# A hybrid decoder layer in float32: the second recurrence column's weights asked for one projection sooner, and two groups of ScalarE instructions bound behind that column's rounding

## The chip, the cores and the metric

The kernel runs on one core of a Trainium2 chip. The metric is the device time of one execution in microseconds; the median of three executions before the change is 1988.41 us (1987.54, 1988.41 and 1988.47).

The engines work side by side and synchronize by semaphores: PE multiplies matrices (and loads weights, PEld), DVE (VectorE), ACT (ScalarE) and POOL (GpSimd) work on elements, SP (SyncE) issues most of the transfers, POOL some. Each engine takes its instructions strictly in its own order: one that waits holds up all that stand behind it there.

## The reference

One layer of a decoder trunk over 1024 tokens and 16 meta tokens, width 1024, in float32:

```python
h = h + 0.5 * swiglu(rms_norm(h, ffn1_norm[l]), ffn1_w_in[l], ffn1_w_out[l])
u = rms_norm(h, mix_norm[l]) @ w_in[l]
hq, hf, hi, hg, sq, sk, sv = jnp.split(u, ...)
o_hg = hgrn2(hq, hf, hi, hg, lb_all[l], hgrn_out_norm[l], valid)
o_sb = stick_breaking(sq, sk, sv, sb_q_norm[l], sb_k_norm[l], valid)
h = h + jnp.concatenate([o_hg, o_sb], axis=-1) @ w_out[l]
h = h + 0.5 * swiglu(rms_norm(h, ffn2_norm[l]), ffn2_w_in[l], ffn2_w_out[l])
```

What matters here is the projection by `w_in`. Its columns feed a gated linear recurrence with four heads of 128 (query, forget gate, value and output gate) and a stick-breaking attention with eight heads of 64, whose queries and keys are normalized by head:

```python
q = rms_norm(split_heads(q_raw, SB_HEADS), q_gain)
k = rms_norm(split_heads(k_raw, SB_HEADS), k_gain)
z = jnp.einsum('bhqd,bhkd->bhqk', qblk, k) * scale
log_beta = jnp.where(allowed, jax.nn.log_sigmoid(z), -jnp.inf)
log_keep = jnp.where(allowed, jax.nn.log_sigmoid(-z), 0.0)
suffix = lax.cumsum(log_keep, axis=3, reverse=True) - log_keep
w = jnp.exp(log_beta + suffix)
```

## The kernel before

**Products.** A float32 operand is held as two: an upper part, rounded by a cast, and a lower part, the rest. A product is three matmuls (upper by upper, lower weights by upper, upper weights by lower; lines 248 to 250). For a block of 128 columns of `w_in`, `col_tile` and `split_w` issue one transfer on SP (line 226, tile `raw`, two buffers), round it on ScalarE (line 231, `wh`, three buffers) and form the lower part on VectorE (line 233, `wl`, three buffers). The rounding is the `wh` cast; this text calls it the column's rounding.

**The stage.** The attention heads are projected in four pairs, `sb_project` with p from 0 to 3: keys, values and queries of a pair, each in chunks of up to 512 tokens. `sb_qk` then normalizes the pair's queries and keys: squares on ScalarE and sums on VectorE (lines 1424 to 1427), the roots, the products on GpSimd (line 1438), transposes back on VectorE (line 1444), and for each of four pieces `put_split`: the upper part `ohi` on ScalarE (line 1375), the lower part `olo` on VectorE (line 1376), and two writes to DRAM issued by GpSimd (lines 1379 and 1380). `ohi` and `olo` have three buffers each, so the fourth piece waits for the write of the first.

**The recurrence's columns.** `hgrn_fill` projects sixteen columns, for each of four heads in the order v, f, q, g. The first two (v and f of head 0) are computed right behind the fourth pair, in four pieces of 264, 264, 256 and 256 tokens; the others are woven into the attention. A piece of v is copied out by ScalarE (line 1108), a piece of f goes through two sigmoids (lines 1114 and 1115) and two scalings on VectorE (lines 1116 and 1119), a half of q or g through one sigmoid and a product (lines 1122 and 1123). All are staged in the tile `st`, four buffers, and stored by SP (lines 1110, 1120 and 1124). Two PSUM banks take turns for the projections up to f, and one serves from q on.

**The scores.** `sb_jobs` and `sb_scores` work on one head after the other. For a piece of the scores, PE forms `z` (lines 1599 to 1602; two banks), ScalarE takes two sigmoids, `keep` and `sig` (lines 1605 and 1606), VectorE scans `keep` (line 1609) and GpSimd multiplies (line 1615). The tiles of the scores lie in memory that the fourth pair's tiles leave; a first write to such a tile waits for the last reader of what lay there.

**What sets the order.** PE's order is written out by hand (the weaving of `weave` and `braid`). The other engines' instructions are placed by a scheduler from when it expects them to be ready; `issue_after(ins)` binds the instructions of its block that run on the engine of `ins` behind `ins` in that engine's order, without a wait for its end. `project` asks for weights up to two columns ahead (`self.columns`, lines 1069 to 1075) and keeps each rounding in `self.rounds`. The list ends with the first column of the recurrence, so that one's weights are asked for during the fourth pair's value projection. From there `hgrn_fill` asks for one column ahead, when a column begins (line 1134): the second column at the start of the first, the third at the start of the second, and so on. `kept["round"]` (line 1135) is the rounding traced last, and the first column's copies stand behind it (line 1142). The fourth pair's upper parts stand behind `self.rounded`, the rounding traced last when their piece is traced (line 1447).

Of the kernel before, what the change touches and what calls it, by code (L numbers as in the profile page):

```python
# [40 lines left out]
class Block:  # L41
# [1050 lines left out]
    def hgrn_fill(self, xh, xl, pool, dst):  # L1092

        nc = self.nc
        plan, cols = self.heads_plan, self.columns_of_heads()

        def staged(n):
            return pool.tile([P, 512], F32, tag="st", name="st", bufs=4)[:, :n]

        def use(kind, h, ps, c0, n):  # L1100
            s = slice(c0, c0 + n) if kind in "vf" else slice(c0 - META, c0 - META + n)
            t = staged(n)
            if c0 >= HALVES[1][0] and kind != "g":
                ps = ps[:, ::-1]
                at = s.start + HALVES[1][0] + T - 2 * c0 - n
                s = slice(at, at + n)
            if kind == "v":
                nc.scalar.copy(t, ps)  # L1108
                with self.tc.issue_after(self.last_load.ins):
                    nc.sync.dma_start(dst[kind][h, :, s], t)  # L1110
                return
            elif kind == "f":
                k = staged(n)
                nc.scalar.activation(t, ps, AF.Sigmoid)
                nc.scalar.activation(k, ps, AF.Sigmoid, scale=-1.0)
                nc.vector.tensor_scalar(
                    t, t, self.lbc[:, h : h + 1], self.lb[:, h : h + 1], ALU.mult, ALU.add
                )
                nc.vector.tensor_scalar_mul(k, k, self.lbc[:, h : h + 1])
                nc.sync.dma_start(dst["k"][h, :, s], k)  # L1120
            else:
                nc.scalar.activation(t, ps, AF.Sigmoid)
                nc.vector.tensor_mul(t, t, ps)
            nc.sync.dma_start(dst[kind][h, :, s], t)

        def weights(i):
            return self.col_tile(self.a["w_in"][0], cols[i])

        kept = {"next": None}

        def part(i, ci, c0, n, half):
            if ci == 0 and half == 0:
                kept["w"] = kept["next"] or self.ahead_w.pop(cols[0])
                kept["next"] = weights(i + 1) if i + 1 < len(plan) else None
                kept["round"] = self.rounded.ins
            if half == 0:
                kept["ps"] = self.proj_bank(n)
            self.product(
                kept["ps"], kept["w"], xh, xl, c0, n, range(4 * half, 4 * half + 4)
            )  # L1140
            if half == 1:
                with self.tc.issue_after(kept["round"]) if i == 0 else ExitStack():
                    use(*plan[i], kept["ps"], c0, n)

        for i, (kind, _) in enumerate(plan):
            for ci, (c0, n) in enumerate(PIECES if kind in "vf" else HALVES):
                for half in range(2):
                    yield 12 * (n * 0.42 + 13), lambda a=(i, ci, c0, n, half): part(*a)
# [177 lines left out]
    def sb_project(self, p, xh, xl, pool, mix, dst):  # L1326
        nc = self.nc
        vT = pool.tile([P, T], F32, tag="vTs", name="vTs", bufs=2)
        kT = pool.tile([P, T + META], F32, tag="kT", name="kT", bufs=2)
        nc.gpsimd.memset(kT[:, T:], 1.0)  # L1330
        qT = pool.tile([P, SEQ], F32, tag="qT", name="qT", bufs=2)
        def use_q(ps, ci, c0, n):
            s = slice(c0 - META, c0 - META + n)
            nc.scalar.copy(qT[:, s], ps)

        def use_k(ps, ci, c0, n):
            nc.scalar.copy(kT[:, c0 : c0 + n], ps)

        def use_v(ps, ci, c0, n):
            nc.scalar.copy(vT[:, c0 : c0 + n], ps)  # L1340

        w = None
        if p == 0:
            w, self.ahead_w, self.rounds = self.early_w, {}, {}
            self.columns = [c + P * i for i in range(1, 4) for c in (2560, 3072, 2048)]
            self.columns.append(self.columns_of_heads()[0])
            for use, x, ci in ((use_k, "k", 0), (use_v, "v", 1), (use_v, "v", 2), (use_v, "v", 0),
                               (use_k, "k", 1), (use_k, "k", 2)):
                use(self.early[x][ci], ci, *CHUNKS[ci])
            use_q(self.early["q"][0], 0, *CHUNKS[0])  # L1350
            self.after_early()
        else:
            yield from self.project(xh, xl, 2560 + P * p, CHUNKS, use_k)
            yield from self.project(xh, xl, 3072 + P * p, CHUNKS, use_v)
        done = [self.sb_v(p, vT, mix, dst[2]), self.sb_qk(p, qT, kT, pool, mix, dst)]
        rest = self.project(xh, xl, 2048 + P * p, HALVES[: 1 if p == 0 else 2], use_q, w)
        if p == 0:
            yield next(rest)
        yield "start", done[0]
        yield from rest  # L1360
        yield "start", done[1]
        return done
# [47 lines left out]
    def sb_qk(self, p, qT, kT, pool, mix, dst):  # L1410
# [31 lines left out]
        for src, c0, b0, nb in rows:  # L1442
            t = src[:, c0 : c0 + 32 * nb]
            nc.vector.transpose(t, nat[:, b0 : b0 + nb].rearrange("p b d -> p (b d)"))
            n = min(32 * nb, (SEQ if src is qT else T) - c0)
            gain, to = (self.qg8, dst[0]) if src is qT else (self.kg, dst[1])
            with self.tc.issue_after(self.rounded.ins) if p == 3 else ExitStack():
                self.put_split(to, p, slice(c0, c0 + n), t[:, :n], mix, gain)
            yield 0, 1500

# [888 lines left out]
```

## Time and profile before

| | |
|---|---|
| median of three executions | 1988.41 us (1987.54 to 1988.47) |
| the profiled execution, device time | 1989.4 us |
| its span, from the first instruction to the last | 1987.7 us |
| granted TensorE clock, mean over the span | 0.998 |
| HBM read and written | 233.75 MB and 111.38 MB |
| 835 to 865 us: busy PE, DVE, ACT, POOL of 30 us | 28.52, 14.42, 13.49, 7.08 |
| 860 to 895 us: busy PE, DVE, ACT, POOL of 35 us | 27.25, 24.14, 21.76, 12.91 |
| 895 to 1180 us: busy PE, DVE, ACT, POOL of 285 us | 276.68, 200.22, 171.65, 106.34 |

Times within the span count from its first instruction. A row of the timeline has start, duration, engine, line, operation, the tile written and the tile read, and in brackets how long the engine was idle before it and what ended that. A wait is put down to the one that came last. The span and the device time differ by 1.7 us in the profiled execution; differences of the span can be carried over to the device time.

The stage of the change lies between 800 and 905 us. The fourth pair's values are projected up to 826 us, its queries up to 837.5, the v column from there on, the f column up to 862.3, and the first scores follow.

### The profile page before, as it was taken

The numbers are of one execution on the slowest core, as the hardware profiler recorded it, in microseconds if no ns is written. First come the engines' busy times: TensorE is split into PE (matmuls) and PEld (weight loads), VectorE is DVE, ScalarE is ACT, GpSimd is POOL, SyncE is SP. The second block draws the span as 40 slices with busy tenths as digits, with TensorE's granted clock in tenths as the row PEclk, the third lists the DMA queues.
The fourth block names the chain that finished last, engine by engine and source line by source line (L and its number), as shares of the span: only waits on it lengthen the run. The fifth ranks groups of instructions, "written<-read, shape, count | busy, mean of one in ns | idle before, by whom it ended". The sixth has DMA issues, their size and how long they took to land.

```text
span 1987.7 us, 30439 instructions
## 1 busy us (share of the span) xinstructions
PE 1938.9 (98%) x10768; PEld 1631.7 (82%) x10768; DVE 1390.3 (70%) x2176; ACT 854.7 (43%) x1719; POOL 449.4 (23%) x616
## 2 busy tenths in 40 slices
PE   7999999999999999989999999899999999999998
PEld 6888888888888888878898978787888888888887
DVE  7977777877677765567777676567566766767774
ACT  6523443334444444456666635433233332344443
POOL 3010100010000003133333332220544544520000
PEclk9999999999999999999999999999999999999999
DMA  7366887758966225664454176665523323278463
GB/s 209 92 169 166 254 272 242 238 183 317 374 207 185 93 73 150 154 191 135 127 152 117 58 264 184 149 228 181 185 96 106 107 96 111 102 266 301 122 197 138
DMA packets 346168, 347.16 MB, mean 175 GB/s; under 512 B 94800, under 2 KB 250320, under 8 KB 346016
## 3 DMA queue, kind: packets, MB, share of 16 engines
q1 hardware_dynamic: 325168, 283.73, 46.5%
q0 software_dynamic: 19808, 61.49, 8.9%
q8 instruction: 85, 1.39, 0.3%
q14 instruction: 67, 0.55, 0.1%
q10 hardware_dynamic: 1040, 0.00, 0.0%
HBM read 233.75 MB, written 111.38 MB: 174 GB/s over the span
## 4 chain that ended last, share of the span: by engine, by line
PE 89%; DVE 4%; DMA 3%; ACT 2%; issue 1%; POOL 1%; SPq 0%; DVEq 0%; ACTq 0%; POOLq 0%
PE o L723 21%; PE qb L448 18%; PE qa L448 12%; PE qc L448 12%; PE proj L248 4%; PE proj L250 4%; PE proj L249 4%; PE flip L1454 2%; PE wo L248 1%; PE wo L249 1%; PE wo L250 1%; PE mq L992 1%; PE oacc L1529 1%; PE oacc L1531 1%; PE z L1599 1%
## 5 line engine op out<-in xcount | busy, mean ns | idle before, releaser
L448 PE MATMUL qb<-T,wh 128*128 128x512 f32 x1056 | 344.6, 390 | 1.4 <-ACT T L308 0.8
L448 PEld LDWEIGHTS qb<-T,wh 128*128 128x128 f32 x1056 | 198.1, 188 | 46.3 <-issue 2.5
L448 PE MATMUL qa<-B,wh 128*128 128x512 f32 x696 | 226.9, 391 | 0.0
L248 PE MATMUL proj<-xh,wh 128*128 128x512 f32 (+2 forms) x640 | 213.5, 334 | 2.6 <-ACT st L1108 1.5
L723 PE MATMUL o<-t,w 128*128 128x512 f32 x924 | 211.9, 390 | 0.5 <-DVE u L541 0.5
L250 PE MATMUL proj<-xl,wh 128*128 128x512 f32 (+2 forms) x640 | 209.8, 328 | 0.8 <-DVE xl L1918 0.8
L723 PE MATMUL o<-parts 128*128 128x512 f32 x924 | 209.9, 389 | 0.0
L249 PE MATMUL proj<-xh,wl 128*128 128x512 f32 (+2 forms) x640 | 209.7, 328 | 0.0
L448 PE MATMUL qb<-T,wl 128*128 128x512 f32 x528 | 205.4, 389 | 0.0
L723 PEld LDWEIGHTS o<-t,w 128*128 128x128 f32 x924 | 172.7, 188 | 37.4 <-issue 0.8
L723 PEld LDWEIGHTS o<-parts 128*128 128x128 f32 x924 | 173.3, 188 | 36.0
L361 DVE TENSOR_TENSOR wl<-s,wh 128x512 fp32r<-128x512 f32 x160 | 165.5, 1034 | 52.1 <-ACT wh L359 51.2
L359 ACT CAST wh<-s 128x512 fp32r<-128x512 f32 x160 | 99.4, 622 | 194.2 <-PE qb L448 150.7
L448 PEld LDWEIGHTS qa<-B,wh 128*128 128x128 f32 x696 | 130.8, 188 | 27.3 <-DVE B L827 0.3
L359 ACT CAST wh<-raw 128x512 fp32r<-128x512 f32 x120 | 74.4, 621 | 148.3 <-PE qc L448 106.6
L448 PE MATMUL qa<-B,wl 128*128 128x512 f32 x348 | 135.6, 390 | 0.0
L248 PEld LDWEIGHTS proj<-xh,wh 128*128 128x128 f32 x640 | 120.6, 188 | 14.7 <-ACT st L1108 1.7
L250 PEld LDWEIGHTS proj<-xl,wh 128*128 128x128 f32 x640 | 120.4, 188 | 12.2 <-DVE xl L1918 1.2
L249 PEld LDWEIGHTS proj<-xh,wl 128*128 128x128 f32 x640 | 120.5, 188 | 9.9
L448 PE MATMUL qc<-B,wh 128*128 128x512 f32 x352 | 115.0, 390 | 2.1 <-DVE u L541 2.1
L448 PE MATMUL qc<-T,wh 128*128 128x512 f32 x352 | 116.9, 394 | 0.0
L448 PEld LDWEIGHTS qb<-T,wl 128*128 128x128 f32 x528 | 99.1, 188 | 20.2
(398 smaller groups left out, 3871.8 us busy)
## 6 DMA issues: line engine op xcount, KB each, us to landing
raw<-in_ffn_w_in_dram SPq DMA_DIRECT2D x176, 256.0 KB, 4.0
raw<-in_ffn_w_out_dram SPq DMA_DIRECT2D x112, 256.0 KB, 4.3
w2in<-both SPq DMA_DIRECT2D x28, 512.0 KB, 3.4
raw<-in_w_in_dram SPq DMA_DIRECT2D x25, 512.0 KB, 4.8
ks<-kD SPq DMA_DIRECT2D x32, 260.0 KB, 5.0
wout<-both SPq DMA_DIRECT2D x16, 512.0 KB, 4.0
wh<-w2in SPq DMA_DIRECT2D x27, 256.0 KB, 3.2
wl<-w2in SPq DMA_DIRECT2D x27, 256.0 KB, 3.4
```

Of the source, the lines that this page charges most:

```text
L248: nc.tensor.matmul(ps, wh[:, s], xs, start=k == 0, stop=False)
L249: nc.tensor.matmul(ps, wl[:, s], xs, start=False, stop=False)
L250: nc.tensor.matmul(ps, wh[:, s], xl[:, k, c0 : c0 + n], start=False, stop=k == nk - 1)
L359: nc.scalar.copy(hi, src)
L361: nc.vector.tensor_sub(lo, src, hi.bitcast(F32))
L448: nc.tensor.matmul(ps, a[:, k, :], b[:, k, :], start=start and k == 0 and i == 0, stop=k == 3 and i == 2, skip_group_check=True,)
L723: nc.tensor.matmul(banks[bank][m], y[:, m * P : (m + 1) * P], z, start=start and at == 0 and e == 0, stop=q == nq - 1 and e == 2, skip_gro ...
L992: nc.tensor.matmul(ps[at : at + 32, at_g, :], self.xm[:, 4 * h + k, :], got[i, h][:, k, :], start=h == 0 and kk == 0, stop=h == 1 and kk = ...
L1454: self.nc.tensor.transpose(ps[:m, j, :], src[:, s0 : s0 + m], self.ident)
L1529: nc.tensor.matmul(o[:, c], vj, w[0], start=j == 0, stop=False, skip_group_check=True)
L1531: nc.tensor.matmul(o[:64, c], vj[:, :64], w[1], start=False, stop=end, skip_group_check=True)
L1599: nc.tensor.matmul(z, q, ks[0][:, s0 : s0 + n], start=True, stop=False)
```

## The change

```diff
-        def weights(i):
-            return self.col_tile(self.a["w_in"][0], cols[i])
-
-        kept = {"next": None}
+        kept = {}
 
         def part(i, ci, c0, n, half):
             if ci == 0 and half == 0:
-                kept["w"] = kept["next"] or self.ahead_w.pop(cols[0])
-                kept["next"] = weights(i + 1) if i + 1 < len(plan) else None
-                kept["round"] = self.rounded.ins
+                kept["w"] = self.ahead_w.pop(cols[i])
+                for c in cols[i + 1 : i + (3 if i == 0 else 2)]:
+                    if c not in self.ahead_w:
+                        self.ahead_w[c] = self.col_tile(self.a["w_in"][0], c)
+                kept["round"] = self.rounds[cols[1]]
...
-            self.columns.append(self.columns_of_heads()[0])
+            self.columns += self.columns_of_heads()[:2]
...
-            with self.tc.issue_after(self.rounded.ins) if p == 3 else ExitStack():
+            with self.tc.issue_after(self.rounds[self.columns[-1]]) if p == 3 else ExitStack():
                 self.put_split(to, p, slice(c0, c0 + n), t[:, :n], mix, gain)
```

The list of columns to load ahead now has the first two columns of the recurrence, so the second column's weights are asked for during the fourth pair's query projection. At the start of the first column the third is asked for; from the third column on, each asks for the next one, as before. The first column's copies stand behind the second column's rounding, and so do the fourth pair's upper parts, since the last of `self.columns` is the second column.

No instruction is added or removed on PE, GpSimd, VectorE, ScalarE or SP; PE's and GpSimd's orders are the same, and the other three change in this stage alone. Line numbers after 1126 are one lower in the changed kernel.

ScalarE, from the fourth pair's last query copy to the table load of the sigmoids. `sq` are the squares of the norms, `sbo` and `sbs` their sums and roots, `raw` and `wh` a column's weights, `st<-proj` from line 1108 the copies of the v column. Before:

```order
L1334 COPY qT<-proj 128x512 x2
L1426 ACTIVATE sq_8250<-nat 128x512
L1426 ACTIVATE sq_8288<-nat 128x512
L1426 ACTIVATE sq_8329<-nat 128x512
L1426 ACTIVATE sq_8363<-nat 128x544
L1430 COPY sbo<-sbs 32x65 x4
L1434 ACTIVATE sbs<-sbs,eps 128x65
L1396 CAST vhl<-vt 128x32
L231 CAST wh<-raw 128x1024
L1108 COPY st<-proj 128x264 x2
L1108 COPY st<-proj 128x256 x2
L1114 ACT_TABLE_LOAD
```

The same place now, up to the third of the copies:

```order
L1333 COPY qT<-proj 128x512 x2
L231 CAST wh<-raw 128x1024
L1425 ACTIVATE sq_8256<-nat 128x512
L1425 ACTIVATE sq_8294<-nat 128x512
L1108 COPY st<-proj 128x264
L1425 ACTIVATE sq_8335<-nat 128x512
L1425 ACTIVATE sq_8369<-nat 128x544
L1429 COPY sbo<-sbs 32x65 x4
L1108 COPY st<-proj 128x264
L1433 ACTIVATE sbs<-sbs,eps 128x65
L1374 ACTIVATE ohi<-qT,qg_82 128x512
L1108 COPY st<-proj 128x256
```

The second column's rounding has moved ahead of the squares, the copies of v stand between the steps of the norm, and the first upper part stands ahead of the table load.

ScalarE, around the f column's sigmoids (`st<-proj`, lines 1114 and 1115), up to the first score piece (`keep` and `sig`). Before:

```order
L231 CAST wh<-raw 128x1024
L1375 ACTIVATE ohi<-qT,qg_82 128x512
L1114 ACTIVATE st<-proj 128x256
L1115 ACTIVATE st<-proj 128x256
L1375 ACTIVATE ohi<-qT,qg_82 128x512
L1114 ACTIVATE st<-proj 128x256
L1115 ACTIVATE st<-proj 128x256
L1375 ACTIVATE ohi<-kT,kg 128x512
L231 CAST wh<-raw 128x1024
L1375 ACTIVATE ohi<-kT,kg 128x528
L1605 ACTIVATE keep<-z 128x144
L1606 ACTIVATE sig<-z 128x144
```

Now, from the last upper part to the last two sigmoids of f; `keep` and `sig` follow them directly:

```order
L1374 ACTIVATE ohi<-kT,kg 128x528
L231 CAST wh<-raw 128x1024
L1114 ACT_TABLE_LOAD
L1114 ACTIVATE st<-proj 128x264
L1115 ACTIVATE st<-proj 128x264
L1114 ACTIVATE st<-proj 128x264
L1115 ACTIVATE st<-proj 128x264
L1114 ACTIVATE st<-proj 128x256
L1115 ACTIVATE st<-proj 128x256
L231 CAST wh<-raw 128x1024
L1114 ACTIVATE st<-proj 128x256
L1115 ACTIVATE st<-proj 128x256
```

All four upper parts and the third column's rounding stand ahead of the table load, and the fourth column's rounding stands ahead of the last two sigmoids of f instead of behind them.

VectorE, around the scalings of the f column (`st<-st`), with the lower parts `olo` of the pair and `wl` of the weights. Before:

```order
L233 TENSOR_TENSOR wl<-raw,wh 128x1024
L1376 SCALAR_TENSOR_TENSOR olo<-qT,qg_82,ohi 128x512
L1116 TENSOR_SCALAR st<-st,lbc,lb 128x256
L1119 TENSOR_SCALAR st<-st,lbc 128x256
L1376 SCALAR_TENSOR_TENSOR olo<-qT,qg_82,ohi 128x512
L1116 TENSOR_SCALAR st<-st,lbc,lb 128x256
L1119 TENSOR_SCALAR st<-st,lbc 128x256
L1376 SCALAR_TENSOR_TENSOR olo<-kT,kg,ohi 128x512
L2141 MEMSET idle 128x1
L233 TENSOR_TENSOR wl<-raw,wh 128x1024
L1376 SCALAR_TENSOR_TENSOR olo<-kT,kg,ohi 128x528
L1609 SCALAR_TENSOR_TENSOR keep<-keep,idle 128x144
```

Now:

```order
L1375 SCALAR_TENSOR_TENSOR olo<-kT,kg,ohi 128x528
L233 TENSOR_TENSOR wl<-raw,wh 128x1024
L1116 TENSOR_SCALAR st<-st,lbc,lb 128x264
L1119 TENSOR_SCALAR st<-st,lbc 128x264
L1116 TENSOR_SCALAR st<-st,lbc,lb 128x264
L1119 TENSOR_SCALAR st<-st,lbc 128x264
L1116 TENSOR_SCALAR st<-st,lbc,lb 128x256
L1119 TENSOR_SCALAR st<-st,lbc 128x256
L233 TENSOR_TENSOR wl<-raw,wh 128x1024
L1116 TENSOR_SCALAR st<-st,lbc,lb 128x256
L1119 TENSOR_SCALAR st<-st,lbc 128x256
L2140 MEMSET idle 128x1
```

The last lower part and the third column's lower part stand ahead of all scalings of f, and the fourth column's lower part stands ahead of the last two.

On SP, the second column's load now directly follows the first column's, the third column's stands ahead of the first store of v, and the fourth column's stands behind the second store of the forget gate, as before.

## The prediction

> **What bounds the kernel now.** I read the page first, for the bound and the chain that ended last.
>
> ```profile
> span 1987.7 us, 30439 instructions
> PE 1938.9 (98%) x10768; PEld 1631.7 (82%) x10768; DVE 1390.3 (70%) x2176; ACT 854.7 (43%) x1719; POOL 449.4 (23%) x616
> PE 89%; DVE 4%; DMA 3%; ACT 2%; issue 1%; POOL 1%; SPq 0%; DVEq 0%; ACTq 0%; POOLq 0%
> ```
>
> PE is the bound, so the change can only be worth what PE waits for, or runs slowly, at its place. The order of the engines shows that place: between the fourth pair's query projection and the first scores. The view of waits, for PE from 800 to 930 us, gives what there is to win:
>
> ```profile
> PE z L1599 <- ACT sig L1606: 6.5, 4, 5.6
> PE proj L248 <- ACT st L1108: 1.5, 1, 1.5
> PE flip L1454 <- DVE wu L1578: 1.3, 1, 1.3
> ```
>
> The timeline of PE puts the two long waits at 843.51 to 845.00 and at 865.84 to 871.42 (start, duration, then in brackets the idle time before it):
>
> ```profile
> 845.00 0.38 PE L248 MATMUL proj<-xh,wh 128*128 128x256 f32 x1 [1.49 <-ACT st L1108]
> 856.60 0.28 PE L248 MATMUL proj<-xh,wh 128*128 128x256 f32 x1
> 862.49 0.47 PE L248 MATMUL proj<-xh,wh 128*128 128x512 f32 x1
> 871.42 0.75 PE L1599 MATMUL z<-ks,qs 128*128 128x456 f32 x1 [5.58 <-ACT sig L1606]
> 877.60 0.48 PE L248 MATMUL proj<-xh,wh 128*128 128x512 f32 x1
> ```
>
> They are: the third chunk of the v column; the third chunk of the f column; the first half chunk of the q column; the third score piece; the second half chunk of q. The timeline of ScalarE, VectorE and GpSimd tells what PE waited for:
>
> ```profile
> 843.63 1.04 ACT L231 CAST wh<-raw 128x1024 fp32r<-128x1024 f32 x1
> 853.89 1.28 ACT L1114 ACT_TABLE_LOAD   x1 [2.57 <-PE proj L250]
> 858.34 0.73 ACT L1375 ACTIVATE ohi<-qT,qg 128x512 fp32r<-128x512 f32 x1
> 862.75 0.38 ACT L1115 ACTIVATE st<-proj 128x256 f32<-128x256 f32 x1
> 865.53 1.05 ACT L231 CAST wh<-raw 128x1024 fp32r<-128x1024 f32 x1 [1.79 <-DMA raw<-in_w_in_dram]
> 866.49 0.73 ACT L1375 ACTIVATE ohi<-kT,kg 128x528 fp32r<-128x528 f32 x1
> 867.12 0.27 ACT L1605 ACTIVATE keep<-z 128x144 f32<-128x144 f32 x1
> 871.07 0.29 ACT L1606 ACTIVATE sig<-z 128x144 f32<-128x144 f32 x1 [3.68 <-DVE olo L1376]
> 862.31 1.12 POOL L1380 DMA_DIRECT2D qD<-olo  x2
> 870.21 0.77 DVE L1376 SCALAR_TENSOR_TENSOR olo<-kT,kg,ohi 128x528 fp32r<-128x528 f32 x1 [2.37 <-DMA qD<-olo]
> ```
>
> The first wait: the copies of the v chunks stand behind the second column's rounding, which runs only at 843.63. The second: the fourth pair's upper parts are queued behind the third column's rounding (858.34), so its last lower part comes last on VectorE, waits until the write issued at 862.31 gives its buffer back, and holds the first sigmoid of the scores (its tile lies where kT lay) until 871.07. ScalarE meanwhile had stood free for 2.57 us before 853.89.
>
> **Part by part.** *First wait.* The second column is now loaded one projection sooner and rounded right behind the second query copy, at about 838.2; the first v copy follows two squares later, at about 841, before PE wants its bank at 843.51. The wait of 1.49 goes: **-1.49**. The price is that the fourth pair's norms come later: VectorE now forms that column's lower part ahead of their sums.
>
> ```profile
> 838.96 2.91 DVE L1427 TENSOR_REDUCE sbs<-sq 128x16 f32<-128x512 f32 x4
> 849.27 1.22 DVE L233 TENSOR_TENSOR wl<-raw,wh 128x1024 fp32r<-128x1024 f32 x1
> 844.37 4.13 POOL L1438 TENSOR_TENSOR nat<-nat,sbs 128x512 f32<-128x512 f32 x4 [23.69 <-DVE sbs L1435]
> ```
>
> Rounding to 839.25, lower part to 840.5: the sums start at 840.5 and not at 838.96, 1.55 later, and so does all behind them. GpSimd ends its products at 850.05 (844.37 + 4.13 + 1.55).
>
> *The upper and lower parts of the fourth pair.* They now run where ScalarE and VectorE stood free, but the fourth upper part needs the first one's buffer, so it waits for a write; behind it on ScalarE stand the third column's rounding, the table load and the f sigmoids. The third pair, which went through this already, gives the price:
>
> ```profile
> 814.03 1.12 POOL L1379 DMA_DIRECT2D qD<-ohi  x2
> 816.91 0.74 ACT L1375 ACTIVATE ohi<-kT,kg 128x528 fp32r<-128x528 f32 x1 [2.00 <-DMA qD<-ohi]
> 815.14 1.08 POOL L1380 DMA_DIRECT2D qD<-olo  x2
> 819.07 0.77 DVE L1376 SCALAR_TENSOR_TENSOR olo<-kT,kg,ohi 128x528 fp32r<-128x528 f32 x1 [0.41 <-DMA qD<-olo]
> DMA to landing us min/median/max: 2.7/3.6/8.5
> ```
>
> From issue to the fourth upper part 2.88 (814.03 to 816.91): 850.05 + 2.88 = 852.93. Then 0.74, the rounding 1.05, the table load 1.28, two sigmoids of 0.38 less overlaps: the first f chunk's bank is free at about 856.75. PE, 1.49 sooner, wants it at 855.11 (856.60 - 1.49). A **new wait of 1.65**. The last row (these writes, 740 to 870 us) bounds it: at 2.7 it is 1.5, at 8.5 it is 7.3. I take the third pair's price; it is the same instruction, before the queues fill.
>
> *The q column.* It starts when PE ends f (862.49 + 1.65 - 1.49 = 862.65) and the third f chunk's bank is free.
>
> ```profile
> 855.61 0.42 DVE L1116 TENSOR_SCALAR st<-st,lbc,lb 128x264 f32<-128x264 f32 x1 [5.12 <-ACT st L1114]
> 856.69 3.75 DMA hg_f<-st
> 859.58 0.46 SPq L226 DMA_DIRECT2D raw<-in_w_in_dram  x1
> DMA to landing us min/median/max: 3.6/5.0/7.4
> ```
>
> VectorE's last lower part waits for the first one's write: 850.05 + 1.12 + 3.93 (815.14 to 819.07) = 855.1; with 0.77 and the third column's lower part 1.22 it scales the first f chunk from 857.0. From scaling to landing took 855.61 to 860.44, 4.83: 861.8, then the third chunk's sigmoid 0.38: 862.2. Covered by 0.4 us, **0**; without that cover each microsecond of the write counts in full.
>
> *The third score piece.* SP asks for the fourth column's weights behind the second f store, at about 859.0 (before 859.58), and its rounding now stands in front of the last two f sigmoids and the first score piece. Landing took 5.95 (859.58 to 865.53); the median of these transfers from 740 to 930 us, the last row above, is 5.0. I take 5.4, since the pair's eight writes of about 256 KB have left that stretch: 864.4, rounding 865.45, two sigmoids 866.15, keep and sig 866.7. PE is there at 866.0 (862.65 + 3.35, as from 862.49 to the wait's start at 865.84). The wait of 5.58 falls to 0.7: **-4.9** (0.3 at 5.0, 2.7 at 7.4). What is late next is this load, no longer a write.
>
> *The scores behind it.* From the third piece to the second half of q took 6.18 (871.42 to 877.60), at half the clock:
>
> ```profile
> 835.00:865.00 30.00, 28.52 (x218) 27.39 (x217) 14.42 (x26) 13.49 (x29) 7.08 (x10) 1.00 0.45 111
> 871.40:877.60 6.20, 5.77 (x19) 3.67 (x19) 5.03 (x6) 4.77 (x13) 3.61 (x9) 0.52 1.00 311
> 872.71 0.55 ACT L1605 ACTIVATE keep<-z 128x456 f32<-128x456 f32 x1 [0.77 <-PE z L1602]
> 876.76 0.46 ACT L1605 ACTIVATE keep<-z 128x348 f32<-128x348 f32 x1 [0.33 <-PE z L1600]
> ```
>
> (The windows' columns: stretch, length, busy time of PE, PEld, DVE, ACT and POOL, then granted clock, DMA share, GB/s.) Two banks alternate, and ScalarE idles for 0.77 and 0.33 us because the slow PE brings pieces late. The wait of 1.49 left the clock at 1.00, the wait of 5.58 was followed by 0.52. With waits of 1.65 and 0.7 the clock stays, and ScalarE's idle time mostly goes: **-1.0** (0 to -1.4).
>
> The Trainium skill, TensorE: Matmul & The Clock Gate, Part 1, says that the clock halves after an idle window of about 3.4 us and comes back after about as long a busy one. Both waits here agree with its bound; its recovery is shorter than the 6.2 us at 0.52 above. By its figure the half clock would have cost at most 1.7 us.
>
> *Given back.* VectorE starts the scans behind the fourth column's lower part and two scalings, at about 867.6 and not 871.96: 4.4 sooner, where PE is 5.7 sooner. Up to 1.3 us may return where PE waited for VectorE (the 1.3 in the waits above): **+0.4**. The rest of the recurrence's queue keeps its order, but for a few roundings and loads that have slack.
>
> Sum: -1.49 + 1.65 + 0 - 4.9 - 1.0 + 0.4 = **-5.3 us**. The profiled execution took 1989.4 us, 1.7 around its span of 1987.7, and would take 1984.1; the median of the three runs is 1988.41, 1.0 below it. So I predict **1983.1 us**.
>
> **Rivals.** *The gain is eaten behind the stage.* The scans bound the first heads (VectorE 13.72 of 17.40 us busy from 877.6 to 895), and PE waits there for the 1.3 that it is ahead, while the load of the fourth column takes its 7.4 (2.0 more). Then -5.3 + 0.9 + 2.0 = -2.4: 1986.0. For it: the load now stands in front of three things on ScalarE. Against it: VectorE has idle time there.
>
> *Slower.* The first upper part's write takes 8.5, as the longest did. ScalarE is held 5.6 longer in front of the f sigmoids, PE waits 7.3 at the third f chunk, and the clock falls there: at 0.52 for 6.2 us it loses 3.0. Then the score wait vanishes: -1.49 + 7.3 + 3.0 - 5.58 - 1.0 + 0.4 = +2.6: 1991.0. It decides from about 5.7 us on, where the wait passes 4 us and the clock's loss joins it. Against it: the long ones ran from 860 to 872, with the engines full; from 835 to 865 their share is 0.45.
>
> *A table switch that costs more than its load.* If the engine also stood still around the load for as long as the load takes (1.28 at 853.89), the new wait would be 1.3 longer, of which 0.7 is covered by the wait for the fourth column: -4.7, 1983.7.
>
> ```profile
> 741.51 0.76 ACT L1430 COPY sbo<-sbs 32x65 f32<-32x65 f32 x3
> 742.29 1.28 ACT L1434 ACT_TABLE_LOAD   x1
> ```
>
> Here copies end at 742.27 and the load starts at 742.29, so nothing is added. The Trainium skill, ScalarE: Activation LUTs, What ACT_TABLE_LOAD costs, gives 1.38 of draining beside the load for every switch, by which the time would be 1983.8; the row does not bear that out.
>
> *It doesn't do what it says.* The parts stay late, because a wait and not the order held them: 1988.4. Against it: the norms' products were done at 848.50, and the first upper part ran at 858.34.
>
> **How the numbers follow.** The forecast has 0.66, the eaten gain 0.22, slower 0.07, the table 0.03, no effect 0.02. The range takes the bounds: at best no wait is left for the scores (-0.7), the clock's term is 1.4 (-0.4), and nothing is given back but the later wait of 1.3 goes (-1.7): -8.1, 1980.3. Upwards it reaches through the eaten gain to -1.2: 1987.2. The forecast's own range is 1981.0 to 1985.0. About 0.2% (4.0 us) is what a measurement of this kernel can tell from no change. The forecast lies 1.3 beyond it. Faster: 0.63 (0.60 of the forecast, the table's 0.03). Within: 0.31 (0.05 of the forecast, 0.20 of the eaten gain, 0.04 of the slower case, 0.02 for no effect). Slower: 0.06 (what is left of the three, for sizes beyond those named).
>
> **What would show it.** Right: no wait of PE for the v copies near 843; a wait of 1 to 2 us ahead of f's third chunk, behind the first f sigmoid; the fourth upper part near 853 and the last lower part near 856; a score wait under 1.5 us, behind a rounding that waited for its load; granted clock 1.00 throughout. Wrong: a wait of more than 4 us at the third f chunk, with a clock near 0.5 behind it; the fourth column's rounding later than 867; or PE's lead at the second half of q (about 5.7 us) gone by 900.

## The result, and the profile after

| | before | changed |
|---|---|---|
| device time, median (lowest to highest) | 1988.46 us (1987.54 to 1988.88, 5 runs) | 1980.80 us (1979.72 to 1983.31, 5 runs) |
| ratio to before, 95% interval | | 0.9963 (0.9949 to 0.9977) |
| the profiled execution: device time, span | 1989.4, 1987.7 us | 1979.72, 1978.0 us |
| granted clock, mean | 0.998 | 0.999 |

The change makes the kernel faster by 0.37% (0.23 to 0.51%). The forecast was 1983.1, with a range of 1980.3 to 1987.2: the median lies in it, 2.3 us below the forecast and 0.5 above its lower end. It is 0.2 us below the forecast's own, narrower range (1981.0 to 1985.0).

First the page of the changed kernel, its span, PE's row and the chain that ended last:

```profile
span 1978.0 us, 30441 instructions
PE 1936.5 (98%) x10768; PEld 1630.9 (82%) x10768; DVE 1390.0 (70%) x2176; ACT 854.9 (43%) x1719; POOL 447.0 (23%) x616
PE 90%; DVE 4%; DMA 2%; ACT 2%; issue 1%; POOL 1%; SPq 0%; DVEq 0%; ACTq 0%; POOLq 0%
```

PE does the same 10768 matmuls, 2.4 us shorter in sum, and the span is 9.7 shorter. Most of what went is idle time of PE. The view of waits of the changed kernel, PE from 800 to 930 us, in which 6.5 and 1.5 us stood before:

```profile
PE proj L248 <- ACT st L1115: 1.3, 1, 1.3
PE z L1598 <- ACT sig L1605: 1.1, 4, 0.5
PE flip L1453 <- DVE wm L1577: 0.5, 1, 0.5
PE flip L1453 <- DVE wu L1577: 0.4, 1, 0.4
```

The wait for the v copies is gone, the long wait for the scores is gone, and one new wait stands there, of 1.3. The timeline of PE shows it, and the places where I measure:

```profile
855.79 0.39 PE L248 MATMUL proj<-xh,wh 128*128 128x256 f32 x1 [1.28 <-ACT st L1115]
861.57 0.23 PE L1598 MATMUL z<-ks,qs 128*128 128x144 f32 x1
864.98 0.48 PE L1598 MATMUL z<-ks,qs 128*128 128x456 f32 x1
869.86 0.48 PE L248 MATMUL proj<-xh,wh 128*128 128x512 f32 x1
885.17 0.31 PE L1598 MATMUL z<-ks,qs 128*128 128x144 f32 x1
1092.28 0.23 PE L1598 MATMUL z<-ks,qs 128*128 128x144 f32 x1
```

They are: f's third chunk; the first score piece; the third score piece; the second half chunk of q; the first score piece of the second head, and that of the last head. ScalarE in the changed kernel; its first row is the table load ahead of the stage, at 742.29 before:

```profile
741.63 1.28 ACT L1433 ACT_TABLE_LOAD   x1
...
852.07 0.74 ACT L1374 ACTIVATE ohi<-kT,kg 128x528 fp32r<-128x528 f32 x1 [1.94 <-DMA qD<-ohi]
852.72 1.03 ACT L231 CAST wh<-raw 128x1024 fp32r<-128x1024 f32 x1
853.77 1.28 ACT L1114 ACT_TABLE_LOAD   x1
855.06 0.39 ACT L1114 ACTIVATE st<-proj 128x264 f32<-128x264 f32 x1
857.27 0.39 ACT L1115 ACTIVATE st<-proj 128x264 f32<-128x264 f32 x1 [1.25 <-DMA hg_v<-st]
862.96 1.05 ACT L231 CAST wh<-raw 128x1024 fp32r<-128x1024 f32 x1 [2.42 <-DMA raw<-in_w_in_dram]
```

And VectorE, GpSimd and SP there (from their timelines):

```profile
839.88 2.72 DVE L1426 TENSOR_REDUCE sbs<-sq 128x16 f32<-128x512 f32 x4
849.26 1.11 POOL L1378 DMA_DIRECT2D qD<-ohi  x2
858.84 0.43 SPq L226 DMA_DIRECT2D raw<-in_w_in_dram  x1
```

The chain of the new wait can be read downwards: the first upper part's write, issued at 849.26, lets the fourth upper part go at 852.07; the third column's rounding, the table load and the first sigmoids follow without a gap; PE goes on at 855.79. The fourth column's load, issued at 858.84, lets its rounding go at 862.96, before PE needs anything that stands behind it. The clock, in the windows (stretch, length, busy time of PE, PEld, DVE, ACT, POOL, then granted clock, DMA share, GB/s):

```profile
835.00:865.00 30.00, 28.72 (x221) 27.54 (x219) 15.16 (x25) 15.73 (x33) 8.58 (x15) 1.00 0.56 168
868.00:880.00 12.00, 11.31 (x65) 8.90 (x64) 9.70 (x16) 7.71 (x23) 6.21 (x9) 1.00 0.87 218
```

The half clock of 871.4 to 877.6 is not there any more.

**A ruler for small differences.** Executions of one kernel spread over 1.3 to 5 us, and much of that lies far from the change: the stretch between the two last table loads of the profile took 123.71 us before, 123.20 in the changed kernel, and 122.89 to 126.01 in the kernels below, though no edit touches it. So I measure each profile from the table load ahead of the stage to the last head's first score piece. Before, that is 742.29 to 1100.95:

```profile
862.27 0.23 PE L1599 MATMUL z<-ks,qs 128*128 128x144 f32 x1
893.63 0.52 PE L1454 MATMUL flip<-ident,sig 128*128 128x128 f32 x3 [1.29 <-DVE wu L1578]
893.91 0.32 PE L1599 MATMUL z<-ks,qs 128*128 128x144 f32 x1
1100.95 0.23 PE L1599 MATMUL z<-ks,qs 128*128 128x144 f32 x1
```

358.66 us before and 350.65 in the changed kernel (1092.28 - 741.63): -8.01. A second profile of the changed kernel (below) gives 350.58. Cut at the places above:

| stretch | before | changed | difference | forecast |
|---|---|---|---|---|
| table load to the first score piece | 119.98 | 119.94 | -0.04 | +0.16 (-1.49 + 1.65 + 0) |
| first to third score piece | 9.15 | 3.41 | -5.74 | -4.9 |
| third piece to q's second half | 6.18 | 4.88 | -1.30 | -1.0 |
| q's second half to the second head | 16.31 | 15.31 | -1.00 | +0.4 |
| second head to the last | 207.04 | 207.11 | +0.07 | 0 |
| sum | 358.66 | 350.65 | -8.01 | -5.3 |

### The profile page after: what moved, and what is told of

It reads as the page before. It is cut to its first block, busy times and chain, and to the rows that moved or that the text cites. A ratio compares the mean times of both kernels' runs of the same rounds, so it can differ in the third digit from the quotient of the medians.

```text
span 1978.0 us, 30441 instructions
## 1 busy us (share of the span) xinstructions
PE 1936.5 (98%) x10768; PEld 1630.9 (82%) x10768; DVE 1390.0 (70%) x2176; ACT 854.9 (43%) x1719; POOL 447.0 (23%) x616
## 4 chain that ended last, share of the span: by engine, by line
PE 90%; DVE 4%; DMA 2%; ACT 2%; issue 1%; POOL 1%; SPq 0%; DVEq 0%; ACTq 0%; POOLq 0%
PE o L723 21%; PE qb L448 18%; PE qa L448 12%; PE qc L448 12%; PE proj L248 5%; PE proj L250 4%; PE proj L249 4%; PE flip L1453 2%; PE wo L249 1%; PE wo L248 1%; PE wo L250 1%; PE oacc L1528 1%; PE mq L992 1%; PE oacc L1530 1%; PE lvl L1224 1%
```

## The experiments

The stage in this table is the ruler's length; its difference is to the profile of before. Ratios are to runs of the kernel before on the same chip. Its median was 1988.11 us beside four of the kernels (changed again, weights alone, binding alone, last part behind f's sigmoids), 1988.92 beside the last two of the table, and 1988.21 beside the other four.

| kernel | median us (lowest to highest) | ratio to before (95%) | stage | difference |
|---|---|---|---|---|
| changed, again | 1980.73 (1980.67 to 1982.98) | 0.9966 (0.9954 to 0.9979) | 350.58 | -8.08 |
| weights alone | 1982.20 (1979.63 to 1983.08) | 0.9967 (0.9954 to 0.9979) | 353.11 | -5.55 |
| weights alone, again | 1981.52 (1980.36 to 1984.31) | 0.9966 (0.9954 to 0.9979) | 351.12 | -7.54 |
| binding alone | 1983.75 (1982.57 to 1985.80) | 0.9979 (0.9970 to 0.9988) | 352.95 | -5.71 |
| last part behind f's sigmoids | 1980.64 (1979.19 to 1982.48) | 0.9964 (0.9951 to 0.9976) | 350.55 | -8.11 |
| the same, a store on GpSimd | 1979.71 (1978.47 to 1983.44) | 0.9958 (0.9944 to 0.9971) | 350.19 | -8.47 |
| fourth column sooner | 1982.56 (1980.53 to 1984.87) | 0.9972 (0.9962 to 0.9983) | 351.89 | -6.77 |
| two buffers, not three | 1982.22 (1978.83 to 1983.68) | 0.9968 (0.9956 to 0.9979) | 352.27 | -6.39 |
| last part behind f, own buffer | 1979.58 (1978.77 to 1982.29) | 0.9959 (0.9946 to 0.9971) | 349.02 | -9.64 |
| own buffer alone | 1981.86 (1979.42 to 1982.78) | 0.9965 (0.9952 to 0.9977) | 350.55 | -8.11 |

The intervals of the ratios all overlap: by whole times only "faster than before" is settled for each. What follows about single waits is read from the profiles.

### The changed kernel again

> The changed kernel again, for a second profile and for a comparison on the same chip as the kernels below. Theory (the forecast's mechanism: two waits of PE and the half clock behind the longer one are gone): PE waits about 1.3 us ahead of the third f chunk, under 1 us in all for the scores up to the second half of q, and the median lies 6.5 to 8.5 us below the kernel before. Rival (part of the first measurement was luck of one session): the median lies 3 to 5 us below it, and the profile shows a wait of several microseconds in the stage.

No edit. The new wait is 1.34 at f's third chunk, and the stage agrees with the first profile's within 0.07 us, while the whole times of this kernel spread over 2.3 us and more. The ruler doesn't always repeat so well: two profiles of the weights alone, below, differ by 1.99.

### Each part alone

Weights alone (the upper parts bound as before):

```diff
-            with self.tc.issue_after(self.rounds[self.columns[-1]]) if p == 3 else ExitStack():
+            with self.tc.issue_after(self.rounded.ins) if p == 3 else ExitStack():
```

> The changed kernel with the fourth pair's upper parts bound as before, behind the rounding traced last when their pieces are traced (the third column's); the second column's weights are asked for sooner. Theory (each part removes its own wait, and a new wait of the fourth pair's parts against f takes some of it back): no wait at the third v chunk, the upper parts between 851 and 856 us, PE waits 1 to 2 us at the third f chunk and again at the first half of q, no half clock; 3 to 6 us below the kernel before. Rival A (the loads arriving sooner are the whole gain): as much as the changed kernel, 7 to 8 us below. Rival B (the binding is the whole of the second term): only the 1.5 us of the first wait, and the score wait of over 5 us stays.

Binding alone (the kernel before, with each rounding of `weights` kept, so that the upper parts can be bound behind the second column's):

```diff
-            return self.col_tile(self.a["w_in"][0], cols[i])
+            w = self.col_tile(self.a["w_in"][0], cols[i])
+            self.rounds[cols[i]] = self.rounded.ins
+            return w
...
-            with self.tc.issue_after(self.rounded.ins) if p == 3 else ExitStack():
+            with self.tc.issue_after(self.rounds[self.columns_of_heads()[1]]) if p == 3 else ExitStack():
```

> The kernel before with the fourth pair's upper parts bound behind the second column's rounding and nothing else changed; no weights are asked for sooner. Theory: the wait of 1.49 us for the v copies stays; the upper parts run from about 846 us, the fourth waits for the first one's write in front of the last two v copies, so that PE waits 1.5 to 2 us at the start of f; the score wait and the half clock go; 3.5 to 6.5 us below the kernel before. Rival A (the loads are the gain): within 1.5 us of the kernel before. Rival B (the binding alone is the gain): 7 to 8 us below.

Either part alone takes away the long score wait; neither is the whole, and the parts don't add up (-7.54 and -5.71 for -8.01 together). The weights alone leave waits of 0.49 at f's third chunk and 1.21 at the start of q, in the profile without the clock's disturbance (below): 0.4 more than the 1.28 of the changed kernel. I had expected 1 to 2 us at both places and no half clock; the first of the two waits is shorter, and the first profile had a half clock. The binding alone leaves 1.49 ahead of v's third chunk, since the copies of v still stand behind the second column's rounding, and 1.41 ahead of f: the last two of those copies are queued behind the fourth upper part, which waits for its write. PE's timeline of that kernel, and ScalarE's:

```profile
844.50 0.38 PE L248 MATMUL proj<-xh,wh 128*128 128x256 f32 x1 [1.49 <-ACT st L1108]
851.82 0.39 PE L248 MATMUL proj<-xh,wh 128*128 128x264 f32 x1 [1.41 <-ACT st L1108]
...
850.78 0.73 ACT L1377 ACTIVATE ohi<-kT,kg 128x528 fp32r<-128x528 f32 x1 [2.33 <-DMA qD<-ohi]
851.42 0.63 ACT L1108 COPY st<-proj 128x256 f32<-128x256 f32 x2
```

With the weights alone the upper parts are still bound behind the third column's rounding, but that now runs at 848.99 and not at 858.34, since its load was asked for at the start of the first column; all four are out by 853.83 + 0.74 (these times are of the first profile). So most of the gain needs only the loads.

### The weights alone, a second profile

> The kernel with the weights' part alone once more, for its clock. Its first profile had a granted clock of 0.53 from 869.9 to 873.4 us although no wait ahead of it was longer than 1.2 us; the changed kernel had 1.00 there. If that follows from this order of work, it is seen again at the same place and the time is again about 1.5 us above the changed kernel's (1982.2). If it depends on how the waits fall in time, a second profile may show 1.00 there, and the span is then about 1.5 us shorter than the first one's 1981.4: about 1979.9.

The first profile was 1.99 us longer than this one in the stage. The windows of the first, and then of the second:

```profile
866.73:870.14 3.41, 2.43 (x11) 1.23 (x10) 3.17 (x5) 3.41 (x9) 1.30 (x4) 1.00 0.60 173
870.14:873.56 3.42, 3.42 (x11) 2.61 (x12) 3.21 (x6) 1.88 (x6) 2.23 (x3) 0.50 1.03 215
```

```profile
870.14:873.56 3.42, 3.42 (x20) 2.83 (x20) 3.21 (x5) 1.62 (x6) 2.47 (x3) 1.00 1.01 201
```

The same order of work ran once at half the clock for 3.42 us and once at 1.00. So the order alone doesn't decide it; what does isn't shown. From the third score piece to the second head's first one the two profiles took 21.72 and 20.20 us, so the half clock cost about 1.5 us; the other 0.5 of the 1.99 lies elsewhere in the stage.

### The last upper part behind f's sigmoids

```diff
-                nc.scalar.activation(k, ps, AF.Sigmoid, scale=-1.0)
+                sig = nc.scalar.activation(k, ps, AF.Sigmoid, scale=-1.0)
+                self.first_gate = self.first_gate or sig.ins
...
-            with self.tc.issue_after(self.rounds[self.columns[-1]]) if p == 3 else ExitStack():
+            behind = self.first_gate if b0 == 48 else self.rounds.get(self.columns[-1])
+            with self.tc.issue_after(behind) if p == 3 else ExitStack():
...
+        self.first_gate = None
```

> The changed kernel with the fourth pair's last upper part bound behind the first f chunk's second sigmoid, so that no write is waited for in front of the f sigmoids. Theory (PE's wait at the third f chunk is the fourth upper part's wait for a write, with the third column's rounding and the table load behind it): that wait goes and nothing takes its place before the scores; 1 to 1.5 us below the changed kernel. Rival (the wait moves on to the fourth column's load, which is asked for at the same time as before): PE waits as much more in front of the third score piece; within 0.4 us of the changed kernel.

The wait at f's third chunk went, so it did come from the part that waits for its write. But one chunk further on a wait of the same size stood: PE and ScalarE of this kernel, from their timelines.

```profile
858.10 0.39 PE L248 MATMUL proj<-xh,wh 128*128 128x256 f32 x1 [1.27 <-ACT st L1115]
857.66 0.39 ACT L1115 ACTIVATE st<-proj 128x264 f32<-128x264 f32 x1 [3.18 <-DMA hg_v<-st]
```

The second sigmoid of the second chunk needs a staging buffer, and the store that frees it, of v's fourth chunk, had stood on SP behind four writes of vD. The changed kernel's row at 857.27 shows the same wait, 1.25, hidden there behind the one ahead. A wait with another cause took the place: stage -8.11, no gain.

### That store on GpSimd

On top of the edit above:

```diff
+                if h == 0 and c0 == PIECES[3][0]:
+                    nc.gpsimd.dma_start(dst[kind][h, :, s], t)
+                    return
                 with self.tc.issue_after(self.last_load.ins):
                     nc.sync.dma_start(dst[kind][h, :, s], t)
```

> The kernel with the fourth pair's last upper part behind the first sigmoids of f, and with the store of v's fourth chunk issued by GpSimd instead of SP (there it stood behind four writes of vD; the second sigmoid of f's second chunk waited 3.18 us for it to give its staging buffer back). Theory A: this store was what took the place of the wait that had been removed; then that wait at the fourth chunk of f (1.27) goes, PE reaches the first score piece about 1.3 us sooner, and the time is 1.3 below the changed kernel's: about 1979.4. Rival B: PE is let go and stopped again by the next thing, the fourth column's rounding, whose load still lands 4 us after its issue: a wait of 0.8 to 1.5 at the start of q or at the scores, and no gain, 1980.7.

Half of it: the wait at the fourth chunk went, and one of 0.96 opened at the third. GpSimd and ScalarE of this kernel:

```profile
851.42 0.54 POOL L1110 DMA_DIRECT2D hg_v<-st  x1
855.01 0.39 ACT L1118 ACTIVATE st<-proj 128x264 f32<-128x264 f32 x1 [2.24 <-DMA hg_v<-st]
```

The store now stood behind the pair's first four writes and landed 3.5 us after its issue; and the scheduler had given its buffer to the first chunk's second sigmoid, which needs it sooner. Neither theory put the wait there.

### A buffer of its own for that chunk

```diff
-            t = staged(n)
+            own = kind == "v" and h == 0 and c0 == PIECES[3][0]
+            if not own:
+                t = staged(n)
+            else:
+                t = pool.tile([P, n], F32, tag="st_v", name="st_v", bufs=1)
```

With the last upper part behind f's first sigmoids:

> The kernel with the fourth pair's last upper part behind the first sigmoids of f, and with a buffer of its own for v's fourth chunk, so that no sigmoid of f's first two chunks waits for that chunk's store. The waits of 1.27 (at f's fourth chunk) and 0.96 (at its third) of the two kernels before this one were both ScalarE waiting for a store of v. Theory: with neither write nor store in front of the sigmoids, PE has no wait over 0.3 in the whole f column and comes to the first score piece at about 859.7 and not 861.0; the fourth column's load then is late by 1 to 1.5 in front of the scores. Time 1979.4 to 1980.7, by how much of the lead the load takes back. Rival: the sigmoids wait for the next older store in its place, PE waits 1 us again in the f column, 1980.7.

And on the changed kernel, with nothing else:

> The changed kernel with a buffer of its own for v's fourth chunk, and nothing else. In the changed kernel PE's new wait (1.3 at f's third chunk) stands behind the first chunk's sigmoids, which the write of the first upper part holds, not a store. So the buffer alone should change nothing: the wait of 1.3 stays at the third chunk, the second sigmoid of the second chunk no longer waits 1.0 to 1.3, and the time is 1980.7 within 0.6. Rival: the store is the common cause of both, and the buffer alone takes the wait away: 1979.4.

The single waits came as the theory had it. The buffer alone leaves the wait where it was and the stage at -8.11 (its median, 1981.86, is 0.6 above the upper end of what was expected, 1981.3, within the spread of its runs). PE's timeline:

```profile
856.19 0.38 PE L248 MATMUL proj<-xh,wh 128*128 128x256 f32 x1 [1.31 <-ACT st L1119]
```

Together with the other edit no wait is left in the f column. The view of waits, PE from 800 to 930 us:

```profile
PE z L1604 <- ACT sig L1611: 1.2, 4, 0.5
PE flip L1459 <- DVE wm L1583: 0.5, 1, 0.5
PE flip L1459 <- DVE wu L1583: 0.4, 1, 0.4
PE proj L248 <- ACT kT L1341: 0.2, 1, 0.2
```

The last row is a projection ahead of the stage. PE comes to the first score piece 118.53 us after the table load (860.65 - 742.12), 1.41 sooner than in the changed kernel, and the fourth column's load, which I had expected to be late then, takes nothing of that back: the stage is 1.63 us shorter. So the new wait of the change had two causes, one behind the other, and both must go. This kernel is ahead of the changed one in the stage. Its whole times don't show that: its ratio to before, 0.9959 (0.9946 to 0.9971), can't be told from the changed kernel's, and the execution that was profiled is its slowest (1982.29). In that one the stretch between the two last table loads, far from the stage, took 126.01 us, against 123.20 in the changed kernel's.

### The fourth column's weights sooner

```diff
-                for c in cols[i + 1 : i + (3 if i == 0 else 2)]:
+                for c in cols[i + 1 : i + (3 if i < 2 else 2)]:
```

> The changed kernel, with the fourth column's weights asked for one column sooner (at the start of the second column and not of the third). My prediction named this load as the thing that is late next, with a score wait of 0.7 left. The profile of the changed kernel has no such wait: the load took 4.1 us and not 5.4. If that is so, there is nothing to win here: its rounding runs some 2 to 3 us sooner, PE's waits stay as they are (1.3 at the third chunk of f), 1980.7 within 0.6. Rival: the load still sets the start of the scores through the small waits behind them (0.2 to 0.5 each); then 0.5 to 1.0 us are won. Against both: the load, issued sooner, shares the queues with the pair's writes and makes the wait at the third chunk of f longer, by up to 1 us.

Slower in the stage, and by none of the three ways as I had put them (by whole times it can't be told from the changed kernel). SP, ScalarE and PE of this kernel:

```profile
855.84 0.45 SPq L226 DMA_DIRECT2D raw<-in_w_in_dram  x1
862.08 1.05 ACT L231 CAST wh<-raw 128x1024 fp32r<-128x1024 f32 x1 [3.66 <-DMA raw<-in_w_in_dram]
863.74 0.50 PE L248 MATMUL proj<-xh,wh 128*128 128x512 f32 x1 [0.99 <-ACT st L1115]
```

Issued 3 us sooner (855.84 against 858.84; 3.65 sooner counted from the table load ahead of the stage), the load took 6.2 us and not 4.1, and its rounding now stands in front of the third chunk's sigmoids as well. PE waits 0.99 at the start of q for the bank that these free: the stage is 1.24 longer. The cover at the start of q is gone: I had it at 0.4 us, in the changed kernel it is 1.25 (the third chunk's last sigmoid ends at 860.54, PE starts q at 861.79).

### Two buffers for the parts

```diff
-        bufs = 2 if gain is None else 3
+        bufs = 2
```

> The changed kernel, with two buffers for the upper and the lower parts of queries and keys and not three, so that the third part waits for the first one's write and the fourth for the second one's. If the new wait of 1.3 at f's third chunk is the write plus what is queued behind it, as predicted, the fourth upper part comes about 1 us later, the wait becomes 2 to 2.7, the lower parts and the scalings of f come 0.5 to 1.5 later and a small wait opens at the start of q: 1 to 2 us slower than the changed kernel, 1982 to 1982.7; the third pair, ahead of it, may add up to 1 us. Rival: the writes queue behind one another and one takes 5 us or more, the slower case of the prediction: a wait above 4, the clock near 0.5 behind it, 1986 or more. Second rival: the table load and not the write sets it; then no change.

The wait at f's third chunk is 2.27, as the theory of the write had it (2 to 2.7); none opened at the start of q. ScalarE of this kernel, and then its windows:

```profile
851.40 0.73 ACT L1374 ACTIVATE ohi<-kT,kg 128x512 fp32r<-128x512 f32 x1 [3.02 <-DMA qD<-ohi]
```

```profile
852.88:856.29 3.41, 1.14 (x9) 0.93 (x8) 3.08 (x5) 3.38 (x6) 1.87 (x7) 1.00 0.71 260
856.29:859.70 3.41, 3.41 (x17) 3.41 (x17) 0.86 (x3) 0.42 (x2) 0.00 (x0) 0.50 0.63 219
```

The time came as expected, but not for that reason alone. PE starts f's third chunk only 0.30 later than in the changed kernel (114.46 and 114.16 after the table load), since it had come sooner; the other 1.51 of the 1.81 that it loses up to the first score piece come behind the wait, where half the clock for 3.41 us makes up to 1.7 us.

No run has four buffers for the upper and lower parts, with which the fourth upper part would not have to wait for a write.

## Why the prediction came out

**The first wait, -1.49: right.** No wait is left near 843, and the sums of the norm start at 839.88, or 840.41 on the clock of before (the second query copy ends the projection 0.53 sooner in this profile); I had 840.5.

**The new wait, +1.65: right in place and cause, 0.37 too long.** From the write's issue to the fourth upper part were 2.81 (849.26 to 852.07; I had 2.88). The order of rounding, table load and sigmoids behind it was as forecast. The experiment that moves that part behind the sigmoids shows that the write was the cause. What I did not see is the second wait behind it, for the store of v (1.25 at 857.27), which is why nothing was won there until both were gone.

**The q column, 0: right**, with a cover of 1.25 and not 0.4. The load one column sooner used it up and 1 us of PE's time with it.

**The score wait, -4.9: mis-sized.** It fell to nothing, not to 0.7. The term was the landing of the fourth column's load: I took 5.4 between the median of 5.0 and the 5.95 of that very load before, and it took 4.12 (858.84 to 862.96). The place of the load in the order was right.

**The clock, -1.0: right, measured -1.30**, near the bound of 1.4. But the reason was incomplete. I had written "With waits of 1.65 and 0.7 the clock stays", and let the slower rival have the clock's loss only from a wait of 4 us on. Runs showed a half clock behind a wait of 2.27, and once where no wait was longer than 1.2, so it is in part luck that none followed the new wait of 1.28. In the changed kernel both profiles have 1.00 there. The granted clock of whole executions agrees: its mean was 0.996 to 0.998 in each of the 37 executions of before that ran beside these kernels, and 0.999 or 1.000 in each of the ten of the changed kernel. One stretch of 3.41 us at half clock takes only 0.0009 off such a mean, so one in some of the ten isn't excluded.

**Given back, +0.4: the step that failed.** I took VectorE's queue behind the stage as the same work in the same order, so that PE's lead could only shrink there. It grew by 1.00. First, nothing was given back, because VectorE caught up: it had idle time there (1.33 us at 881.31), and a little later it waits for PE alike in both kernels, 1.97 and 1.98 us. From the table load ahead of the stage that is 7.08 us sooner now (144.58 and 137.50), as much as PE's lead at the second half of q. VectorE before, and in the changed kernel:

```profile
886.87 0.56 DVE L1578 TENSOR_TENSOR wu<-flip,wu 128x384 fp32r<-128x384 f32 x1 [1.97 <-ACT wu L1577]
...
879.13 0.56 DVE L1577 TENSOR_TENSOR wu<-flip,wu 128x384 fp32r<-128x384 f32 x1 [1.98 <-ACT wu L1576]
```

Second, the wait of PE for VectorE ahead of the second head was 1.29 before (893.63) and is 0.38 now (884.84). VectorE and GpSimd before:

```profile
888.49 2.34 DVE L233 TENSOR_TENSOR wl<-raw,wh 128x1024 fp32r<-128x1024 f32 x1 [0.25 <-ACT wh L231]
888.40 1.35 POOL L1615 TENSOR_TENSOR sig<-sig,keep 128x656 f32<-128x656 f32 x1 [3.39 <-DVE keep L1609]
```

And in the changed kernel:

```profile
882.02 1.22 DVE L233 TENSOR_TENSOR wl<-raw,wh 128x1024 fp32r<-128x1024 f32 x1
880.66 1.35 POOL L1614 TENSOR_TENSOR sig<-sig,keep 128x656 f32<-128x656 f32 x1 [3.39 <-ACT keep L1604]
```

A column's lower part ran beside a product of GpSimd before and took 2.34; now it stands two places later in VectorE's order, starts as that product ends (880.66 + 1.35 = 882.01), and takes 1.22. That is 1.12 less in front of what PE waits for. I had waved this move through as one of "a few roundings and loads that have slack". In the kernel with the binding alone that lower part lies outside this stretch, and the wait is 0.38 as well. It is 0.38 too in the profile of the weights alone that has a half clock, so a half clock alone doesn't make it 1.29. The cause is read from traces; no kernel was made for it alone. The best case at the lower end of the range had named this outcome (nothing given back, and the later wait of 1.3 gone), but without a reason for it.

**The rivals.** The parts did not stay late: the first upper part ran at 847.01, not at 858.34. The gain was not eaten behind the stage: from the second head to the last, +0.07 of 8. The slower case did not come: the write took 2.8. The table load, 853.77 to 855.05, is followed by the next sigmoid at 855.06: nothing was added around it. The Trainium skill, ScalarE: Activation LUTs, What ACT_TABLE_LOAD costs, has 1.38 us of draining at each switch; this place doesn't show it, no more than the one quoted in the prediction.

**The sum.** Against the forecast of -5.3 (-5.34 unrounded) the stage gave -8.01, 2.67 more: 0.20 up to the first score piece, 0.84 from the load, 0.30 from the clock, 1.40 from VectorE, less 0.07 behind the second head. The medians differ by 7.66.

## What to carry to other kernels

When a wait is taken away, look for every other thing that the waiting engine needs at that same place (a bank, a buffer, a store that frees it): here two causes stood one behind the other, and removing either alone won nothing. A transfer asked for sooner doesn't always land as much sooner (here 3.65 us became 1.53, both counted from the table load ahead of the stage), and what is bound behind it moves up with it, so the instructions that now stand behind it have to be counted. And where the timing of a stage shifts by several us, look in the next one for pairs of VectorE and GpSimd instructions that will meet or part.

## What the runs showed of the hardware

**The half clock comes in steps of 3.41 us.** It lasted 3.41 us with two buffers (856.29 to 859.70), 3.42 in the first profile of the weights alone (870.14 to 873.56), and before, where it is the only half clock of the span up to PE's last matmul, in its windows:

```profile
867.10:870.51 3.41, 0.00 (x0) 0.00 (x0) 1.04 (x2) 0.29 (x2) 0.54 (x1) 1.00 1.05 312
870.51:873.92 3.41, 2.29 (x6) 1.24 (x6) 2.09 (x4) 2.08 (x6) 1.95 (x8) 0.50 1.03 356
873.92:877.34 3.42, 3.23 (x10) 2.21 (x10) 3.21 (x4) 2.76 (x8) 1.53 (x2) 0.50 0.99 286
```

twice that, 6.83. In the 3.41 us ahead of the fall PE was busy for 0.00, 1.14 and 2.43 us. The Trainium skill, TensorE: Matmul & The Clock Gate, Part 1, describes a window of 3.413 us that runs freely and is not set by the program: the lengths agree, and a window that runs freely fits with one kernel having the fall in one profile and not in the next. It names an idle window as the condition; here windows in which PE worked for a third and for 70% of the time were enough. How much work keeps the clock up is open: in the kernel with the store on GpSimd, 865.00 to 868.41 has the same 2.43 and no fall follows, but where the gate's window lay there isn't known.

**VectorE and GpSimd hold each other up.** The lower part above fits with having waited out the product: 888.40 + 1.35 = 889.75, and from there 1.08 to its end at 890.83, where one alone takes 1.22. The other way round, GpSimd's product of 128x784 took 2.70 us before, beginning (895.17) beside a lower part of 1.20 (895.23), and 1.57 in the changed kernel (886.37), where a lower part starts only 1.20 later. The Trainium skill, SBUF — State Buffer, SBUF: two separate sides, says that such a pair (VectorE with two inputs from SBUF against GpSimd) takes a port in turn, whole instructions at a time; the rows agree with it.
